# Two layers of a convolution-and-attention trunk: half-row transposes, and low weight parts formed by adding transfers

## The chip, the cores and the metric

The kernel runs on one core of a Trainium2 chip. The metric is the device time of one execution in microseconds (us). The kernel before takes 1127.71 us (median of 3 runs, 1127.39 to 1128.07). A change of less than 0.2%, 2.26 us here, cannot be told from no change by these measurements.

## The reference

The reference is a trunk of two layers over 256 latent tokens and 256 context tokens, 1024 channels wide. One input projection feeds three parts: a gated convolution branch (width 31), neighbourhood attention with 8 heads of 64, and sigmoid gates. A gated sum of the branches goes through an output projection, and a gated feed-forward part with a convolution of width 3 follows. In the second layer the context only gives keys and values. Shortened:

```
p = modulate(rmsnorm(x), sh1, sc1) @ w_in            # GLU | q k v | gates
y_conv = swish(layernorm(dwconv31(a * sigmoid(g)))) @ w_conv_out
s = concat(q k_window + bias, q k_ctx) * scale       # rope on latent q, k
y_attn = (softmax(s) @ concat(v_window, v_ctx)) @ w_na_out
x = x + g1 * ((gate_c * y_conv + gate_a * y_attn) @ w_out)
x = x + g2 * (silu(g) * a) @ w_down                  # a, g = dwconv3(h2 @ w_up)
```

## The kernel before, in words

**Weights and products.** Everything is float32 with almost full accuracy. A weight is split into a rounded high part and a low part, and so is each activation; a product then takes three matmuls for each 128 rows of the contraction (`mm3`, L179 high by high, L180 high by the low activation, L181 low by high). Weights come in units of 128 x 1024 elements (512 KB). `wunit` brings one into a buffer `raw` (four of them, SyncE's queue), ScalarE copies it to `whi` (L160) and VectorE subtracts to make `wlo` (L161); there are four `whi` and four `wlo` buffers. `unit8` cuts the unit into eight weight tiles and `group` runs 24 matmuls over it: 512 columns in layer 0 (latent and context), 256 in most of layer 1.

**Order.** TensorE runs its instructions in the order in which the program writes them. After each group `slot()` gives one step to every generator on the list `side`: one issues convolution taps, one steps the attention, one the layer norm, one the adaptive-norm products; `pace` scales how many steps a slot gives to the last kinds. Between units the attention therefore slips its own matmuls.

**Attention.** For two heads (a pair `j`), `products` forms scores (L440): the two heads lie on partitions 0 to 63 and 64 to 127, so each matmul works on 64 rows, and the two of a pair go to two PSUM banks. The tags are `sc`, `sc`, `pt`, `main`. `scores` takes a maximum on VectorE (L458), an exponential on ScalarE (L461) and a scaling (L464); `ctx_scores` does so for the context's queries (L474, L477, L482). `turn` transposes the normalised scores `pp`, 128 x 128 at a time (L494 latent, L499 context), four of them into each of the four banks, and ScalarE copies each bank into `pT` (L495). `values` multiplies `pT` with V (L512). There are six turns in layer 0 (two of them for the context) and four in layer 1. `step` fixes when a turn, values and products are issued: a turn of one step ago, then the values of the turn before it, then the next products.

**Convolution.** `glu` takes a sigmoid on ScalarE (L606) and a product on VectorE into a padded row `u`; 31 taps for each of four channel groups follow on VectorE (L591, in layer 0 124 taps on 512 columns) into `cb`. Layer 0 has two `u` buffers, so `glu` must finish the taps of group j-2 first. `conv_run` issues two taps a slot in layer 0, three in layer 1. `layer_norm` sums the four groups (L842 and L843 on GpSimd, then one addition on VectorE), multiplies by ones on TensorE (L847), and normalises.

Of the kernel before, what the change touches and what calls it, by code (L numbers as in the profile page):

```python
# [8 lines left out]
F32 = mybir.dt.float32  # L9
# [3 lines left out]
ALU = mybir.AluOpType  # L13
# [32 lines left out]
def trunk(ctx: ExitStack, tc: tile.TileContext, xt, cvec, crow, wall, wada, params, bias_t, rope_t, out):  # L46
# [136 lines left out]
    def group(ps, ws, xh, xl, c):  # L183
# [201 lines left out]
    class Attention:  # L385

        def __init__(self, l, eb, T, V, oh, ol):
            self.l, self.eb, self.T, self.V, self.oh, self.ol = l, eb, T, V, oh, ol  # L390
            self.todo, self.soft, self.pv, self.n, self.at = [], [], [], 0, 0
            self.ctx, self.pairs, self.last = [], 0, None

        def pair(self, j, q, k, bt, last):
            self.pairs, self.last = self.pairs + 1, last
# [9 lines left out]

        def ahead(self, j):

            while any(it[0] <= j for _, _, its in self.todo for it in its):
                self.step(True)

        def run(self):
            while True:
# [3 lines left out]
        def step(self, now=False):  # L416
            self.n += 1
            since = self.n - self.at
            if not now and (since < (4 if self.todo else 3 if self.soft else 2) or not self.todo and self.pairs < 4):
                return  # L420
            if self.todo and not now and self.n - self.todo[0][0] < 2:
                return
            self.at = self.n
# [7 lines left out]
            if self.todo:  # L431
                _, what, its = self.todo.pop(0)
                outs = [self.products(it, [psum(t) for t in tags]) for it, tags in zip(its, (("sc", "sc"), ("pt", "main")))]
                self.soft.append((what, its, [(self.scores if what == LAT else self.ctx_scores)(it, o) for it, o in zip(its, outs)]))

        def product(self, out, q, k, c, d):

# [13 lines left out]
        def scores(self, it, out):  # L451
            qt, bt = it[1], it[-1]
            pps = []
            for i, ps in enumerate(out):

                mx = small([P, 1], "mx")
                p2, b2 = ps.rearrange("p (a k) -> p a k", a=2), bt[:, 2 * qt + i :: 4 - 2 * qt - i, :]
                dve.tensor_tensor_reduce(p2, p2, b2, -1.0, 3.0e38, ALU.add, ALU.min, mx)  # L458
                pp = self.eb.tile([P, 512], F32, tag="pp", bufs=4, name=nm("pp"))
                sm = small([P, 1], "sm")  # L460
                self.exp = act.activation(pp, ps, AF.Exp, bias=mx, scale=-1.0, accum_out=sm)  # L461
                ri = small([P, 1], "ri")
                dve.reciprocal(ri, sm)
                self.done = act.mul(pp, pp, ri)  # L464
                pps.append(pp)
            return pps

        def ctx_scores(self, it, out):
            pps = []
            for ps in out:  # L470
                mx = small([P, 2], "mx2")
                dve.tensor_reduce(mx, ps.rearrange("p (q k) -> p q k", q=2), AX.X, ALU.max, negate=True)
# [12 lines left out]

        def turn(self, what, its, pps):

            pts = [self.eb.tile([P, 4, S], F32, tag="pT", bufs=4, name=nm("pT")) for _ in range(2)]
            for n, tags in enumerate((("sc", "sc"), ("pt", "main"))):
                for i, pp in enumerate(pps[n]):  # L490
                    pt = psum(tags[i])
                    if what == LAT:
                        for kt in range(4):
                            pe.transpose(sl(pt, kt), sl(pp, kt), ident)  # L494
                        act.copy(pts[i][:, :, n * P : (n + 1) * P], pt.rearrange("p (k q) -> p k q", k=4))  # L495
                    else:
                        for t in range(2):
                            for kt in range(2):
                                pe.transpose(pt[:, kt * S + t * P : kt * S + (t + 1) * P], sl(pp, 2 * t + kt), ident)  # L499
                        act.copy(pts[i][:, 2 * n : 2 * n + 2, :], pt.rearrange("p (k q) -> p k q", k=2))  # L500
            js = [its[0][0]] if what == LAT else [it[0] for it in its]
            self.pv.append((what, js, pts))

        def values(self, what, js, pts, bank):
            po = psum(bank)
            kts = range(4) if what == LAT else range(2, 4)
            for n, j in enumerate(js):
                c = slice(n * S, (n + 1) * S)
                for kt in kts:
                    for i in range(2):  # L510
                        h = 2 * j + i
                        pe.matmul(  # L512
                            po[i * HD : (i + 1) * HD, c], self.V[kt][:, h * HD : (h + 1) * HD],
                            pts[i][:, 2 * n + kt - kts[0], :], start=kt == kts[0], stop=kt == kts[-1],
                        )
# [42 lines left out]
    for l in range(DEPTH):  # L558
# [5 lines left out]
        with ExitStack() if last else start as e1a:  # L564
# [5 lines left out]
            NU_ = KC if last else 2  # L570
# [10 lines left out]


            taps = []

            def conv_tap(j, t):
                w = par[:, l * NPAR + DW + j * TAPS + t : l * NPAR + DW + j * TAPS + t + 1]
                src = us[j % NU_][:, :, t : t + S]
                if t == 0:
# [4 lines left out]
            rate = [0]  # L593

            def conv_run():
                while True:
                    for _ in range(rate[0]):
                        if taps:
                            conv_tap(*taps.pop(0))
                    yield  # L600
# [32 lines left out]
            with ExitStack() as e1b:  # L633
                eb = e1b.enter_context(tc.tile_pool(name=f"eb{l}", bufs=1))
                V = [eb.tile([P, CONV], F32, name=f"V{l}_{t}") for t in range(4)]
                att = Attention(l, eb, T, V, oh, ol)

                def v_tile(pv, w, k, toks, parts=range(3)):
                    i = k % 2
# [176 lines left out]
            with ExitStack() as e1c:  # L816
# [15 lines left out]
                def layer_norm():  # L832

                    while taps:
# [17 lines left out]
                    yield  # L852
                    yield
# [10 lines left out]
                    pace[0] = 0.4  # L864

                side.remove(conv)
                ln = layer_norm()
# [357 lines left out]
```

## Time and profile before

| | |
|---|---|
| median of 3 runs | 1127.71 us |
| the profiled execution | 1127.64 us |
| its span in the profile | 1125.9 us (1.74 us lie around it) |
| TensorE busy | 1114.1 us, 99% |
| VectorE, ScalarE, GpSimd busy | 908.3, 563.6, 14.7 us |
| granted TensorE clock | 0.998 |
| layer 0: first groups, attention with taps, gates and branches, feed-forward | 0 to 82, 82 to 198, 198 to 320, 320 to 700 us |
| layer 1: attention with taps, the rest | 745 to 870, 870 to 1116 us |

The profile times every instruction of one execution. PE is TensorE's matmuls, PEld its weight loads, DVE VectorE, ACT ScalarE, POOL GpSimd, SP SyncE. In a timeline the first column is the start, the second the duration, and "x6" joins six like instructions; a matmul's duration contains the way through the array, so what a stream of them costs is read from the distance between starts. A tile's name stands without its number.

### The profile page before, as it was taken

What the parts mean: (1) busy time and instruction counts of PE and PEld (TensorE: products, weight loads), DVE (VectorE), ACT (ScalarE), POOL (GpSimd) and SP (SyncE); (2) the same over time, 40 slices, a digit from 0 to 9 for tenths busy, and PEclk for the clock granted to TensorE, in tenths of its full rate; (3) what the DMA queues carried; (4) which work ended last, traced back from release to release, by engine and by line L of the source; (5) the groups of instructions that cost most, each with busy time, mean ns of one, the idle gap of its engine ahead of it and who ended that gap; (6) DMA issues with size and microseconds to landing.
All of it is one profiled execution on the core that took longest, in us unless ns stands there. A gap on an engine that the chain in (4) does not pass through costs nothing.

```text
span 1125.9 us, 17731 instructions
## 1 busy us (share of the span) xinstructions
PE 1114.1 (99%) x6828; PEld 963.0 (86%) x6828; DVE 908.3 (81%) x1631; ACT 563.6 (50%) x934; POOL 14.7 (1%) x24
## 2 busy tenths in 40 slices
PE   9999999999999999999999999999999999999997
PEld 7778777787789988888888888989888999999997
DVE  5689999685778788888898555789996898988773
ACT  4347657542333543434343222544677667766642
POOL 0000000000000000000000000000000000000000
PEclk9999999999999999999999999999999999999999
DMA  9833231536734354554556665556433575565781
GB/s 364 282 94 103 75 118 38 206 97 214 245 118 138 114 161 150 168 169 149 168 171 215 219 191 186 180 181 187 145 126 121 167 250 163 188 194 181 219 268 58
DMA packets 53941, 190.83 MB, mean 169 GB/s; under 512 B 6240, under 2 KB 6496, under 8 KB 53856
## 3 DMA queue, kind: packets, MB, share of 16 engines
q1 hardware_dynamic: 53568, 189.65, 52.1%
q8 instruction: 54, 0.88, 0.3%
q14 instruction: 31, 0.25, 0.1%
q10 hardware_dynamic: 288, 0.04, 0.0%
HBM read 188.62 MB, written 1.05 MB: 168 GB/s over the span
## 4 chain that ended last, share of the span: by engine, by line
PE 83%; DVE 9%; issue 6%; ACT 2%; DMA 0%; POOL 0%; POOLq 0%; DVEq 0%; SPq 0%; ACTq 0%
PE main L179 24%; PE main L181 24%; PE main L180 24%; DVE cb L591 4%; PE main L644 4%; DVE wlo L161 1%; PE sc L181 1%; PE sc L179 1%; PE sc L180 1%; PE po L202 1%; PE po L512 1%; PE sc L129 1%; PE sc L440 0%; DMA sb<-in_crow 0%; PE sc L494 0%
## 5 line engine op out<-in xcount | busy, mean ns | idle before, releaser
L179 PE MATMUL main<-h,whi 128*128 128x256 f32 (+1 forms) x1328 | 446.7, 337 | 0.0
L181 PE MATMUL main<-h,wlo 128*128 128x256 f32 (+1 forms) x1328 | 442.9, 335 | 1.0 <-DVE wlo L161 1.0
L180 PE MATMUL main<-h,whi 128*128 128x256 f32 (+1 forms) x1328 | 442.2, 334 | 0.1
L160 ACT CAST whi<-raw 128x1024 fp32r<-128x1024 f32 (+1 forms) x244 | 252.3, 1039 | 285.5 <-PE main L180 131.5
L161 DVE TENSOR_TENSOR wlo<-raw,whi 128x1024 fp32r<-128x1024 f32 (+1 forms) x244 | 292.9, 1207 | 112.5 <-ACT whi L160 108.0
L179 PEld LDWEIGHTS main<-h,whi 128*128 128x128 f32 x1328 | 249.4, 188 | 32.1 <-issue 3.6
L181 PEld LDWEIGHTS main<-h,wlo 128*128 128x128 f32 x1328 | 249.3, 188 | 29.6 <-DVE wlo L161 1.5
L180 PEld LDWEIGHTS main<-h,whi 128*128 128x128 f32 x1328 | 249.8, 188 | 28.5 <-DVE h L367 0.5
L591 DVE SCALAR_TENSOR_TENSOR cb<-u,par,cb 128x512 f32<-128x512 f32 (+1 forms) x240 | 140.4, 609 | 1.4
L271 DVE CUSTOM_DVE_ANT_0 t<-raw,sb,par 128x1024 bf16<-128x1024 f32 x100 | 126.7, 1277 | 1.0 <-ACT sb L255 0.7
L179 PE MATMUL main<-fh,whi 128*128 128x256 f32 (+1 forms) x386 | 123.0, 319 | 0.0
L180 PE MATMUL main<-fl,whi 128*128 128x256 f32 (+1 forms) x386 | 122.9, 319 | 0.0
L181 PE MATMUL main<-fh,wlo 128*128 128x256 f32 (+1 forms) x386 | 122.9, 318 | 0.0
L180 PEld LDWEIGHTS main<-fl,whi 128*128 128x128 f32 x386 | 72.7, 188 | 5.6
L179 PEld LDWEIGHTS main<-fh,whi 128*128 128x128 f32 x386 | 72.7, 188 | 5.6
L181 PEld LDWEIGHTS main<-fh,wlo 128*128 128x128 f32 x386 | 72.7, 188 | 5.5
L963 ACT ACTIVATE t<-main,par 128x512 f32<-128x512 f32 (+1 forms) x82 | 50.6, 667 | 39.0 <-PE main L181 39.0
L964 DVE SCALAR_TENSOR_TENSOR t<-main,par,t 128x510 f32<-128x510 f32 (+1 forms) x82 | 47.5, 615 | 10.2 <-ACT t L963 9.8
L967 DVE SCALAR_TENSOR_TENSOR t<-main,par,t 128x510 f32<-128x510 f32 (+1 forms) x82 | 46.6, 609 | 0.0
L366 ACT ACTIVATE h<-t,mod 128x256 fp32r<-128x256 f32 x56 | 25.4, 502 | 36.1 <-DVE t L365 36.1
L898 DVE SCALAR_TENSOR_TENSOR x<-main,mod,x 128x256 f32<-128x256 f32 x48 | 22.1, 479 | 23.5 <-PE main L181 23.3
L644 PE MATMUL main<-whi,h 128*128 128x512 f32 x128 | 40.6, 402 | 0.1
(221 smaller groups left out, 1188.2 us busy)
## 6 DMA issues: line engine op xcount, KB each, us to landing
raw<-in_wall SPq DMA_DIRECT2D x239, 512.0 KB, 4.2
raw<-in_wada SPq DMA_DIRECT2D x88, 512.0 KB, 4.3
bias<-in_bias_t SPq DMA_DIRECT2D x8, 640.0 KB, 4.8
row<-in_wada SPq DMA_DIRECT2D x8, 512.0 KB, 4.7
sb<-in_crow SPq DMA_DIRECT2D x5, 512.0 KB, 6.0
x<-in_xt SPq DMA_DIRECT2D x8, 256.0 KB, 4.4
raw<-in_wall SPq DMA_DIRECT2D x8, 256.0 KB, 7.1
out<-t SPq DMA_DIRECT2D x3, 256.0 KB, 2.1
```

Of the source, the lines that this page charges most:

```text
L160: act.copy(hi[:, c], r[:, c])
L161: dve.tensor_tensor(lo[:, c], r[:, c], hi[:, c].bitcast(F32), ALU.subtract)
L179: pe.matmul(ps, w[0], xh, start=start, stop=False)
L180: pe.matmul(ps, w[0], xl, start=False, stop=False)
L181: pe.matmul(ps, w[1], xh, start=False, stop=stop)
L271: dve.tensor_tensor_reduce(tmp().bitcast(BF16), r, v, 1.0, pr(l, BADA + n, 1), ALU.mult, ALU.add, mods[l][:, n, s : s + 1])
L366: high = act.activation(hi[:, c], y[:, c], AF.Identity, bias=b)
L591: dve.scalar_tensor_tensor(cb[j], src, w, cb[j], ALU.mult, ALU.add)
L644: mm = pe.matmul(pv[t], h1[n == 1][k][:, c], w[n == 2][:, b], start=k + n == 0, stop=k == KD - 1 and n == 2)
L963: act.activation(c, pv_, AF.Identity, bias=pr(l, FDB + t, 1), scale=w[1])
L964: dve.scalar_tensor_tensor(c[:, :, 1:], pv_[:, :, : S - 1], w[0], c[:, :, 1:], ALU.mult, ALU.add)
L967: dve.scalar_tensor_tensor(c[:, :, : S - 1], pv_[:, :, 1:], w[2], c[:, :, : S - 1], ALU.mult, ALU.add)
```

## The change

1. *Low parts.* A new `wadded` serves 19 units of layer 0 (the first 19 input-projection units after the first group's) and 7 of layer 1. ScalarE copies the high part as before (L199 in the new file) and writes its negative into `wlo` (L200); GpSimd's queue then issues a DMA that adds `raw` onto `wlo` (L201). VectorE's subtraction falls away for these units.
2. *Turning on row halves.* `turn` issues each transpose as two, one on rows 0 to 63 and one on rows 64 to 127, with 64 columns each, into two PSUM banks (L520 latent and context). A bank now holds one half of both heads, and ScalarE copies two banks (L523) into one `pT` tile.
3. *Order of the attention.* In layer 0 a turn with no values ahead of it stands alone: its products are issued at a later slot (`alone`, `late`).
4. *Tied taps.* Each tap is placed behind the latest maximum (`after`). Layer 0 has four `u` buffers, and three taps a slot.
5. *Sigmoid behind copies.* In layer 0 `glu_groups` first has the attention issue what is ripe, and puts its sigmoid behind the last copy of a turn.
6. *Row sums.* In layer 0 the two additions of L842 and L843 move to VectorE, the pace of the layer norm is 0.6 instead of 1.0 and 0.4, and it yields four times instead of twice behind the squares.
7. The kernel sets a scratch size for descriptors of 1024.

```diff
+ADDED = {*((0, U_IN + i) for i in range(19)), *((1, U_IN + i) for i in (7, 8, 9, 14, 15, 16, 17))}
...
+    def wadded(l, u):
+
+        r = raw_unit(wall[l, u])
+        hi = wp.tile([P, UW], F32R, tag="whi", bufs=4, name=nm("whi"))
+        lo = wp.tile([P, UW], F32R, tag="wlo", bufs=4, name=nm("wlo"))
+        act.copy(hi, r)
+        act.mul(lo, hi.bitcast(F32), -1.0)
+        pool.dma_start(lo, r, accum_op=ALU.add)
+        return hi, lo
...
-        w = wunit(l, u, at)
+        w = wadded(l, u) if (l, u) in ADDED else wunit(l, u, at)
...
+            alone = not self.l and self.soft and not self.pv and not self.late
...
+            if self.late:
+                self.late, self.at = False, self.n
+                return self.issue()
+            if alone and not now:
+                self.late = True
...
-            pts = [self.eb.tile([P, 4, S], F32, tag="pT", bufs=4, name=nm("pT")) for _ in range(2)]
+            pT = self.eb.tile([P, 2, 4, S], F32, tag="pT", bufs=2, name=nm("pT"))
             for n, tags in enumerate((("sc", "sc"), ("pt", "main"))):
+                outs = [psum(t).rearrange("p (i s q) -> p i s q", i=2, s=4) for t in tags]
                 for i, pp in enumerate(pps[n]):
-                    pt = psum(tags[i])
+                    for s in range(4):
+                        src = s if what == LAT else s % 2 * 2 + s // 2
+                        for pt, r in zip(outs, HALF):
+                            pe.transpose(pt[:, i, s], sl(pp, src)[r], ident[r, r])
+                for pt, r in zip(outs, HALF):
                     if what == LAT:
-                        for kt in range(4):
-                            pe.transpose(sl(pt, kt), sl(pp, kt), ident)
-                        act.copy(pts[i][:, :, n * P : (n + 1) * P], pt.rearrange("p (k q) -> p k q", k=4))
+                        self.copied = act.copy(pT[:, :, :, n * P + r.start : n * P + r.stop], pt)
...
             def conv_tap(j, t):
+                if after[0] is not None:
+                    with tc.issue_after(after[0].ins):
+                        tap(j, t)
+                else:
+                    tap(j, t)
...
-                glu(j, pa, pg)
+                copied = None if last else att.ahead(j - 2)
+                with tc.issue_after(copied.ins) if copied else ExitStack():
+                    glu(j, pa, pg)
...
-                rate[0] = 3 if last else 2
+                rate[0] = 3 if last else 3.0
...
-                    pace[0] = 1.0
+                    pace[0] = 1.0 if last else 0.6
...
-                    pool.tensor_tensor(sm[:, :T], flat[0], flat[1], ALU.add)
-                    pool.tensor_tensor(sm[:, :T], sm[:, :T], flat[2], ALU.add)
+                    eng = pool if last else dve
+                    eng.tensor_tensor(sm[:, :T], flat[0], flat[1], ALU.add)
+                    eng.tensor_tensor(sm[:, :T], sm[:, :T], flat[2], ALU.add)
```

**Where instructions move, first place.** TensorE's order at the first turn of layer 0, before: the second unit's last matmuls, the turn, and directly behind it the second pair of products.

```order
L181 MATMUL main_972<-h_189,wlo_975 128x512
L494 MATMUL sc_1009<-ident,pp_845 128x128 x4
L494 MATMUL sc_1015<-ident,pp_853 128x128 x4
L494 MATMUL pt_1021<-ident,pp_861 128x128 x4
L494 MATMUL main_1027<-ident,pp_869 128x128 x4
L440 MATMUL sc_1033<-qk_967,qk_921 128x512
L440 MATMUL sc_1034<-qk_967,qk_921 128x512
```

The same turn after (its first six and last two rows of 32), then a whole unit of 24 matmuls, and only then the products.

```order
L182 MATMUL main_945<-h_189,wlo_949 128x512
L520 MATMUL sc_984<-ident,pp_861 128x64
L520 MATMUL sc_985<-ident,pp_861 128x64
L520 MATMUL sc_984<-ident,pp_861 128x64
L520 MATMUL sc_985<-ident,pp_861 128x64
...
L520 MATMUL pt_1004<-ident,pp_885 128x64
L520 MATMUL main_1005<-ident,pp_885 128x64
L180 MATMUL main_1035<-h_182,whi_1038 128x512
...
L182 MATMUL main_1035<-h_189,wlo_1039 128x512
L465 MATMUL sc_1073<-qk_1030,qk_940 128x512
```

Sixteen transposes have become sixteen pairs with half the columns, whose partners go to different banks, and the turn stands one unit earlier, between two units.

**Second place.** ScalarE's order at the first turn of layer 1, before: three casts of later units and a rotary copy, then the four copies of the turn.

```order
L160 CAST whi_7497<-raw_7496 128x1024
L160 CAST whi_7541<-raw_7540 128x1024
L768 ACTIVATE qk_7333<-t_7327 128x256
L160 CAST whi_7674<-raw_7673 128x1024
L495 COPY pT_7373<-sc_7375 128x4x128
L495 COPY pT_7374<-sc_7381 128x4x128
L495 COPY pT_7373<-pt_7387 128x4x128
L495 COPY pT_7374<-main_7393 128x4x128
```

The same place after: two of the three units are made by adding, so that a negative (L200) follows each of their casts, one of them directly ahead of the copies.

```order
L199 CAST whi_7631<-raw_7629 128x1024
L161 CAST whi_7675<-raw_7674 128x1024
L200 ACTIVATE wlo_7632<-whi_7631 128x1024
L807 ACTIVATE qk_7450<-t_7444 128x256
L199 CAST whi_7824<-raw_7822 128x1024
L200 ACTIVATE wlo_7825<-whi_7824 128x1024
L523 COPY pT_7490<-sc_7491 128x8x64
L523 COPY pT_7490<-sc_7492 128x8x64
L523 COPY pT_7490<-pt_7511 128x8x64
```

One more instruction stands between the cast and the copies, and each copy of an `sc` bank now needs both heads' transposes.

**Third place.** GpSimd's queue in layer 1 after; before, it held only the two additions (L842, L843) here.

```order
L201 DMA wlo_7195<-raw_7192 128x1024
L201 DMA wlo_7233<-raw_7230 128x1024
L201 DMA wlo_7374<-raw_7371 128x1024
L201 DMA wlo_7412<-raw_7409 128x1024
L201 DMA wlo_7594<-raw_7591 128x1024
L882 TENSOR_TENSOR ss_8479<-cb_0_6603,cb_1_6604 128x256
L201 DMA wlo_7632<-raw_7629 128x1024
L201 DMA wlo_7825<-raw_7822 128x1024
L883 TENSOR_TENSOR ss_8479<-ss_8479,cb_2_6605 128x256
```

The seven transfers are interleaved with the two additions of the row sums, in the order in which the queue issues them.

More of the change, by code (lines that the diff above doesn't have):

```diff
@@ L385, in trunk, with __init__ @@
     class Attention:
-        def __init__(self, l, eb, T, V, oh, ol):
+        def __init__(self, l, eb, T, V, oh, ol, after):
+            self.after = after
             self.l, self.eb, self.T, self.V, self.oh, self.ol = l, eb, T, V, oh, ol
             self.todo, self.soft, self.pv, self.n, self.at = [], [], [], 0, 0
-            self.ctx, self.pairs, self.last = [], 0, None
+            self.ctx, self.pairs, self.last, self.late = [], 0, None, False
         def pair(self, j, q, k, bt, last):
@@ L406, in ahead @@
         def ahead(self, j):
+            self.copied = None
             while any(it[0] <= j for _, _, its in self.todo for it in its):
                 self.step(True)
+            return self.copied
         def run(self):
@@ L418, in step @@
             since = self.n - self.at
-            if not now and (since < (4 if self.todo else 3 if self.soft else 2) or not self.todo and self.pairs < 4):
+            alone = not self.l and self.soft and not self.pv and not self.late
+            if not now and since < (4 if self.todo or alone else 3 if self.soft else 2) and not self.late:
                 return
-            if self.todo and not now and self.n - self.todo[0][0] < 2:
+            if not now and not alone and not self.todo and self.pairs < 4:
                 return
+            if not now and not alone and self.todo and self.n - self.todo[0][0] < 2:
+                return
+            if self.late:
[3 more added lines that the diff above has]
+                self.late = True
             self.at = self.n
@@ L430, in step, with issue @@
                 self.values(*work, "sc" if work[0] == CTX and not (soft or self.todo) else "po")
[L431 to L434, printed above, removed]
+            if self.todo and not self.late:
+                self.issue()
+        def issue(self):
+            _, what, its = self.todo.pop(0)
+            outs = [self.products(it, [psum(t) for t in tags]) for it, tags in zip(its, (("sc", "sc"), ("pt", "main")))]
+            self.soft.append((what, its, [(self.scores if what == LAT else self.ctx_scores)(it, o) for it, o in zip(its, outs)]))
         def product(self, out, q, k, c, d):
@@ L486, in turn, with values @@
         def turn(self, what, its, pps):
-            pts = [self.eb.tile([P, 4, S], F32, tag="pT", bufs=4, name=nm("pT")) for _ in range(2)]
+            pT = self.eb.tile([P, 2, 4, S], F32, tag="pT", bufs=2, name=nm("pT"))
             for n, tags in enumerate((("sc", "sc"), ("pt", "main"))):
+                outs = [psum(t).rearrange("p (i s q) -> p i s q", i=2, s=4) for t in tags]
                 for i, pp in enumerate(pps[n]):
-                    pt = psum(tags[i])
+                    for s in range(4):
[3 more added lines that the diff above has]
+                for pt, r in zip(outs, HALF):
                     if what == LAT:
-                        for kt in range(4):
-                            pe.transpose(sl(pt, kt), sl(pp, kt), ident)
-                        act.copy(pts[i][:, :, n * P : (n + 1) * P], pt.rearrange("p (k q) -> p k q", k=4))
-                    else:
[L497 to L500, printed above, removed]
+                        self.copied = act.copy(pT[:, :, :, n * P + r.start : n * P + r.stop], pt)
+                    else:
+                        to = pT[:, :, 2 * n : 2 * n + 2].rearrange("p i k (t q) -> p i (k t) q", t=2)
+                        self.copied = act.copy(to[:, :, :, r], pt)
             js = [its[0][0]] if what == LAT else [it[0] for it in its]
-            self.pv.append((what, js, pts))
-        def values(self, what, js, pts, bank):
+            self.pv.append((what, js, [pT[:, i] for i in range(2)]))
+        def values(self, what, js, pT, bank):
             po = psum(bank)
@@ L513, in values @@
                             po[i * HD : (i + 1) * HD, c], self.V[kt][:, h * HD : (h + 1) * HD],
-                            pts[i][:, 2 * n + kt - kts[0], :], start=kt == kts[0], stop=kt == kts[-1],
+                            pT[i][:, 2 * n + kt - kts[0]], start=kt == kts[0], stop=kt == kts[-1],
                         )
@@ L569, in trunk @@
             rope = ea.tile([P, 2, S], F32, name=f"rope{l}")
-            NU_ = KC if last else 2
+            NU_ = KC
             us = [ea.tile([P, NS, S + 2 * PAD], F32, name=f"u{l}_{i}") for i in range(NU_)]
@@ L583, in trunk, with tap @@
             taps = []
+            after = [None]
             def conv_tap(j, t):
+                if after[0] is not None:
[3 more added lines that the diff above has]
+                    tap(j, t)
+            def tap(j, t):
                 w = par[:, l * NPAR + DW + j * TAPS + t : l * NPAR + DW + j * TAPS + t + 1]
@@ L591, in conv_tap @@
                     dve.scalar_tensor_tensor(cb[j], src, w, cb[j], ALU.mult, ALU.add)
-            rate = [0]
+            rate = [0.0]
             def conv_run():
+                due = 0.0
                 while True:
-                    for _ in range(rate[0]):
+                    due += rate[0]
+                    while due >= 1:
+                        due -= 1
                         if taps:
@@ L635, in trunk @@
                 V = [eb.tile([P, CONV], F32, name=f"V{l}_{t}") for t in range(4)]
-                att = Attention(l, eb, T, V, oh, ol)
+                att = Attention(l, eb, T, V, oh, ol, after)
                 def v_tile(pv, w, k, toks, parts=range(3)):
@@ L851, in layer_norm @@
                         s2.add(flat[j], j == KC - 1)
-                    yield
-                    yield
+                    for _ in range(2 if last else 4):
+                        yield
                     pb = yield from rstd(s2, CONV, "po")
@@ L863, in layer_norm @@
                         yield
-                    pace[0] = 0.4
+                    pace[0] = 0.4 if last else 0.6
                 side.remove(conv)
```

6 lines of the change are left out of this document (3 added, 3 removed).

## The prediction

> **What bounds the kernel now.** I read the busy shares first, then what TensorE waits for, then the busy time by stage, and last the distances between matmul starts. The page's busy line:
>
> ```profile
> span 1125.9 us, 17731 instructions
> PE 1114.1 (99%) x6828; PEld 963.0 (86%) x6828; DVE 908.3 (81%) x1631; ACT 563.6 (50%) x934; POOL 14.7 (1%) x24
> ```
>
> The reader should see that TensorE (PE) is busy for all but 11.8 us. The view of waits, for TensorE's queue, complete:
>
> ```profile
> PE sc L129 <- POOL ident masks.py:199: 1.8, 1, 1.8
> PE main L181 <- DVE wlo L161: 1.0, 2, 0.6
> PE pt L1094 <- DVE t L314: 0.7, 1, 0.7
> PE po L1102 <- DVE rs L1099: 0.6, 1, 0.6
> PE pt L228 <- ACT t L221: 0.6, 1, 0.6
> PE po L351 <- POOL rs L346: 0.4, 1, 0.4
> ```
>
> These are 5.1 us in seven waits, and the only one on a low part made by VectorE is 1.0 us. Two stretches of attention, of layer 0 and layer 1, the columns being PE, PEld, DVE, ACT, POOL, clock, DMA share, GB/s:
>
> ```profile
> 82.00:100.00 18.00, 18.00 (x84) 14.13 (x83) 17.62 (x43) 11.77 (x21) 0.00 (x0) 1.00 0.22 78
> 810.00:830.00 20.00, 20.00 (x144) 16.85 (x142) 20.00 (x53) 15.20 (x31) 0.00 (x0) 1.00 0.52 161
> ```
>
> VectorE is full there, but so is TensorE, and TensorE hardly waits: VectorE's filling is convolution taps, which nothing needs soon. So taking work off VectorE is worth little, at most the 1.0 us of the second row above. What moves the time is **how long TensorE's own list takes**, and that list changes only in the turns.
>
> **The turn, before.** TensorE in layer 1's first turn:
>
> ```profile
> 809.56 0.39 PE L181 MATMUL main<-h,wlo 128*128 128x512 f32 x1
> 809.79 1.04 PE L494 MATMUL sc<-ident,pp 128*128 128x128 f32 x8
> 810.66 0.60 PE L494 MATMUL pt<-ident,pp 128*128 128x128 f32 x4
> 811.10 0.60 PE L494 MATMUL main<-ident,pp 128*128 128x128 f32 x4
> 811.63 1.16 PE L440 MATMUL sc<-qk,qk 64*128 64x512 f32 x6
> ```
>
> Eight transposes take 810.66 - 809.79 = 0.87 us, 0.109 us each; sixteen take 1.74 us, and ten turns 17.4 us. That is all that halving can act on.
>
> **What a half pair costs.** The weight loads by form (busy us, then mean ns):
>
> ```profile
> L494 PEld LDWEIGHTS sc<-ident,pp 128*128 128x128 f32 x64 | 7.4, 141 | 0.8
> L440 PEld LDWEIGHTS main<-qk,qk 64*128 64x128 f32 x36 | 6.0, 185 | 0.2
> L512 PEld LDWEIGHTS po<-pT,V 128*64 128x64 f32 x144 | 9.5, 136 | 5.4 <-issue 1.3
> L179 PEld LDWEIGHTS main<-h,whi 128*128 128x128 f32 x1328 | 249.4, 188 | 32.1 <-issue 3.6
> ```
>
> Loads of 128 and 64 columns take 188 and 136 ns, so 52 ns for 64 columns and some 84 ns fixed. 64 rows with 128 columns take 185: half the rows do not shorten a load. A transpose's load, 141 ns, is 57 ns above the fixed part. A half transpose keeps its 128 weight columns (some 57 ns) and has 64 moving columns instead of 128 (half of 109, 55 ns). So a pair costs about 0.059 us if its two halves run beside each other, twice that if not. Whether they do, the context products show, which are pairs of 64 rows with loads of 64 x 128:
>
> ```profile
> 114.75 0.28 PE L440 MATMUL main<-qk,qk 64*128 64x256 f32 x1
> 114.75 0.28 PE L440 MATMUL pt<-qk,qk 64*128 64x256 f32 x1
> 114.87 0.28 PE L440 MATMUL main<-qk,qk 64*128 64x256 f32 x1
> 114.87 0.28 PE L440 MATMUL pt<-qk,qk 64*128 64x256 f32 x1
> ...
> 115.35 0.28 PE L440 MATMUL main<-qk,qk 64*128 64x256 f32 x1
> ```
>
> Both start together, a pair each 0.12 us. The two loads (185 - 84 = 101 ns each) fit into 0.12 us only side by side. No row shows transposes so, nor a pair closer than 0.12 us; the ends are 0.055 (half of 0.109) and 0.12 us. I take **0.059**, since both resources that I could read give it. Saved: 16 x (0.109 - 0.059) = 0.80 a turn, **8.0 us in ten**. The ends give +8.6 and -1.8.
>
> By the Trainium skill, TensorE: Matmul & The Clock Gate, section "Wait — 56ns, not 53.3ns?", starts are never closer than about 25 ns, and with a sequencer that decodes in software about 62 ns a matmul bind instead. By the first a pair could be 0.05 and the sum stands; by the second it would be 0.124, the case of the first rival below. The rows above, two matmuls in 0.12 us, exclude neither.
>
> **Changing between whole array and halves.** Layer 0's first products, between two units:
>
> ```profile
> 81.67 0.39 PE L180 MATMUL main<-h,whi 128*128 128x512 f32 x1
> 81.90 0.40 PE L181 MATMUL main<-h,wlo 128*128 128x512 f32 x1
> 82.23 0.97 PE L440 MATMUL sc<-qk,qk 64*128 64x512 f32 x6
> 83.04 0.39 PE L440 MATMUL main<-qk,qk 64*128 64x512 f32 x1
> ...
> 83.83 0.50 PE L179 MATMUL main<-h,whi 128*128 128x512 f32 x1
> 84.16 0.40 PE L180 MATMUL main<-h,whi 128*128 128x512 f32 x1
> ```
>
> From 81.90 to 84.16 are eight steps (a whole one, six pairs, a whole one), at the undisturbed 0.23 us (81.67 to 81.90) 1.84 us; 2.26 are spent, so some 0.2 us to enter and 0.2 to leave. Before, a turn was whole and its products had to enter; now the turn enters. Where values (whole rows) stand between turn and products, both now enter. I count 0.25 us for nine turns and 0.2 for layer 0's first, which now stands alone: **-2.4 us** (ends: 0, if the short matmuls hide it, and 10 x 0.4 = 4).
>
> **Copies behind a negative.** ScalarE at layer 1's first turn:
>
> ```profile
> 809.76 1.05 ACT L160 CAST whi<-raw 128x1024 fp32r<-128x1024 f32 x1 [1.35 <-PE main L180]
> 810.71 1.06 ACT L495 COPY pT<-sc 128x512 f32<-128x512 f32 x2
> 811.66 0.60 ACT L495 COPY pT<-pt 128x512 f32<-128x512 f32 x1
> ```
>
> The cast waits for a weight buffer that the last L180 before the turn frees. After, the negative follows it. I price it as a second cast, 1.05 us (no row shows it; at 0.6, a copy's, the wait is half a us shorter). The `sc` copies then run 811.85 to 812.90 instead of to 811.77. The products, which write the `sc` banks, are ready at 809.79 + 0.2 + 16 x 0.059 = 810.9 and wait some 2.0 us: **-1.9 us**, once. Layer 0's turns have the same order, but there either a unit of 24 matmuls (5.5 us) or the values cover the copies; -0.2 together. If all four turns of layer 1 stalled so, it would be -6.
>
> **Adding transfers.** The tightest unit is the second of layer 1's seven in TensorE's order, number 7 of the list. Its cast before, and the first row of its successor, 24 matmuls later:
>
> ```profile
> 779.85 1.05 ACT L160 CAST whi<-raw 128x1024 fp32r<-128x1024 f32 x1 [0.37 <-PE main L180]
> 788.35 0.28 PE L179 MATMUL main<-h,whi 128*128 128x256 f32 x1
> 788.59 0.28 PE L181 MATMUL main<-h,wlo 128*128 128x256 f32 x1
> 791.19 0.39 PE L179 MATMUL main<-h,whi 128*128 128x512 f32 x1
> ```
>
> 788.35 to 788.59 are two steps of 0.12 us, and 24 of them before 791.19 the unit begins, at 788.35, so its first L181 is that at 788.59; the cast ended at 780.90. After the negative (781.95), 6.6 us remain for the transfer. No row shows an adding one, or any issued by GpSimd. The page's nearest, with KB and us to landing:
>
> ```profile
> raw<-in_wall SPq DMA_DIRECT2D x239, 512.0 KB, 4.2
> ```
>
> Plain 512 KB take 4.2 us; two reads for one write make 8.4 the upper end. I take 6 (between them, nearer to the plain row): nothing waits. At 8.4 this unit is 1.8 us late. Layer 0's units have over 12 us each. By the Trainium skill, DMA: Bandwidth & Descriptors, section "Anatomy of one DMA — SWDGE (gpsimd) path", a transfer of GpSimd takes about 2.0 us plus its bytes at 436 GB/s, an estimate of 3.2 us here; by that nothing waits either, and no run here shows it.
>
> **The rest.** VectorE loses 26 subtractions of 1.2 us and gains two additions of about 0.65 us; ScalarE gains 26 x 1.05 us where it is a third idle. Tied taps, three taps a slot, the sigmoid and the row sums reorder work that TensorE does not wait for; I cost them at nothing, hidden by TensorE's units. Of the 1.0 us on `wlo` and the 0.6 us behind `t L221`, in the table of waits, I count a third as gone with the freer VectorE: **+0.5**.
>
> **Sum.** +8.0 - 2.4 - 1.9 - 0.2 + 0.5 = +4.0 us saved. Against the profiled execution, 1127.64 us (span 1125.9 and 1.74 around it), that is **1123.6 us**; the median, 1127.71, stands 0.07 higher.
>
> **Rivals.**
>
> 1. *Half transposes are no cheaper in pairs* (slower side). Each matmul costs a fixed 0.055 to 0.06 us of issue, as the closest rows (ten in 0.60 us) allow. A pair then takes 0.109 to 0.12: the 8.0 becomes 0 to -1.8, and the entering and the copies remain: 1131.6 to 1133.4, say **1132**. It decides from a pair of 0.084 us on, where 160 x 0.025 = 4.0 is used up. Against it: both loads and streams, read by themselves, need under 0.06. If partners even ran one after another at 0.109, it would be 17 us more, 1149.
> 2. *Late adds.* At 8.4 us or more that unit waits 1.8 us, and with VectorE full and transfers queued it could be 10 us, so 3.4 for it and 1 to 2 for the units next to it: 1125.5 to 1129, **about 1127.5**: no change.
> 3. *More gain.* If entering costs nothing where the matmuls are short, and the copies wait less (a negative of 0.6 us), 2.4 + 0.5 more: **about 1120.5**.
> 4. *The change does not do what it says*: adds or halves run as before. The halves are in TensorE's list, so this is only the case of rival 1.
>
> **Chances and range.** Forecast (1121.5 to 1125.4) 0.50; rival 3, below it, 0.13; rival 2, 0.15, spread over no change; rival 1, 0.19; others, 0.03. Faster by over 0.2% (under 1125.4; 2.26 us is about what the measurement can tell) 0.64, within 0.2% 0.16, slower 0.20. The range leaves out the farthest of rivals 1 and 3: 1119.5 to 1132.
>
> **What would show it.** In the changed profile: starts of half transposes of one bank 0.059 us apart (0.11 refutes the largest term); a gap of 0.1 us in front of each turn; in layer 1's first turn a gap of some 2 us on TensorE behind the transposes, ended by the copy L523; TensorE's waits on `wlo` without a row for L201's transfers; transfers of 512 KB from GpSimd's queue in about 6 us. The forecast is wrong if partners do not overlap, or if these transfers take over 8 us.

## The result, and the profile after

The changed kernel takes 1125.12 us (median of 9 runs, 1124.23 to 1126.18) against 1127.71 us before (9 runs, 1127.2 to 1128.42). The ratio is 0.9977, with a 95% interval of 0.9967 to 0.9987: faster by 0.23%, on the edge of what can be told. The profiled execution takes 1124.46 us, with a span of 1122.7 us and a clock of 0.998. The busy line and the waits of TensorE, after:

```profile
span 1122.7 us, 18139 instructions
PE 1110.2 (99%) x6988; PEld 955.8 (85%) x6988; DVE 887.7 (79%) x1607; ACT 588.9 (52%) x960; POOL 36.5 (3%) x50
```

```profile
PE sc L130 <- POOL ident masks.py:199: 1.8, 1, 1.8
PE main L182 <- DVE wlo L162: 1.8, 3, 0.8
PE sc L465 <- ACT pT L523: 1.0, 2, 0.8
PE pt L1134 <- DVE t L325: 0.7, 1, 0.7
PE po L1142 <- DVE rs L1139: 0.6, 1, 0.6
```

VectorE is busy for 20.6 us less, ScalarE for 25.3 us more. TensorE has a new wait, 1.0 us on the copies of two turns (L523), and waits longer on low parts that VectorE makes. Nothing waits on an adding transfer; the page's row for them, KB and us to landing:

```profile
wlo<-raw POOLq DMA_DIRECT2D x26, 512.0 KB, 5.6
```

Layer 1's first turn, TensorE's timeline:

```profile
807.97 0.40 PE L182 MATMUL main<-h,wlo 128*128 128x512 f32 x1
808.29 0.71 PE L520 MATMUL sc<-ident,pp 64*128 64x64 f32 x16
808.84 0.22 PE L520 MATMUL main<-ident,pp 64*128 64x64 f32 x1
808.84 0.22 PE L520 MATMUL pt<-ident,pp 64*128 64x64 f32 x1
808.90 0.22 PE L520 MATMUL main<-ident,pp 64*128 64x64 f32 x1
808.91 0.23 PE L520 MATMUL pt<-ident,pp 64*128 64x64 f32 x1
...
809.31 0.71 PE L465 MATMUL main<-qk,qk 64*128 64x512 f32 x2
810.83 1.22 PE L465 MATMUL sc<-qk,qk 64*128 64x512 f32 x5 [0.81 <-ACT pT L523]
```

Partners start together, and a pair follows each 0.06 to 0.07 us (eight pairs from 808.29 to 808.84). The turn is entered 0.32 us behind the last full matmul instead of 0.23. Over the ten turns, from the matmul ahead to the one behind, a turn took 2.07 us before (0.23 + 1.64 + 0.20, first to last start in the middle) and takes 1.47 us where values follow (0.33 + 0.99 + 0.15). **That is 0.60 us a turn.** The second turn of layer 0 is the exception: it takes 1.33 us in the middle, because it waits inside for a scaled score. ScalarE beside layer 1's first turn:

```profile
808.16 1.05 ACT L199 CAST whi<-raw 128x1024 fp32r<-128x1024 f32 x1 [0.30 <-PE main L181]
809.24 1.06 ACT L200 ACTIVATE wlo<-whi 128x1024 fp32r<-128x1024 f32 x1
810.21 1.06 ACT L523 COPY pT<-sc 128x512 f32<-128x512 f32 x2
```

Cast, negative and copies follow one another, and the products of the `sc` banks start behind the first copy, at 810.83, with the turn over since 809.3. Two products ran ahead, since `main` has four banks.

Where the time came from: the same weight load of the three-matmul products (there are 5796 in both traces) was looked up in both, and its start after is set against its start before.

```
stretch (times of before)                     us after less us before
six turns of layer 0, to 196                  -2.2
a wait of TensorE at 209, gone                -0.8
210 to 351: gates, branches, low parts late   +1.3
layer 1's first turn                          +0.9
layer 1's other three turns                   -1.8
a wait at 937, gone                           -0.3
the end, behind the last weight load          -0.3
sum                                           -3.2
```

Ten turns would be -6.0. Layer 0's six gave -2.2 instead of -3.6, since the second and the third gave nothing, and layer 1's first cost 0.9 instead of giving 0.6.

### The profile page after: what moved, and what is told of

Same layout as the page of the kernel before. It is cut to its first block, busy times and chain, and to the rows that moved or that the text cites. A ratio compares the mean times of both kernels' runs of the same rounds, so it can differ in the third digit from the quotient of the medians.

```text
span 1122.7 us, 18139 instructions
## 1 busy us (share of the span) xinstructions
PE 1110.2 (99%) x6988; PEld 955.8 (85%) x6988; DVE 887.7 (79%) x1607; ACT 588.9 (52%) x960; POOL 36.5 (3%) x50
## 4 chain that ended last, share of the span: by engine, by line
PE 88%; issue 5%; DVE 4%; ACT 2%; POOL 0%; POOLq 0%; DVEq 0%; ACTq 0%
PE main L180 25%; PE main L182 25%; PE main L181 25%; PE main L683 4%; DVE cb L625 2%; PE po L538 1%; PE sc L182 1%; PE sc L180 1%; PE sc L181 1%; PE po L213 1%; PE sc L465 1%; PE sc L130 1%; PE sc L213 0%; PE pt L465 0%; PE sc L520 0%
## 5 line engine op out<-in xcount | busy, mean ns | idle before, releaser
L161 ACT CAST whi<-raw 128x1024 fp32r<-128x1024 f32 (+1 forms) x218 | 225.3, 1037 | 256.6 <-DMA raw<-in_wall 137.4
L162 DVE TENSOR_TENSOR wlo<-raw,whi 128x1024 fp32r<-128x1024 f32 (+1 forms) x218 | 262.2, 1208 | 98.9 <-ACT whi L161 96.9
L625 DVE SCALAR_TENSOR_TENSOR cb<-u,par,cb 128x512 f32<-128x512 f32 (+1 forms) x240 | 144.2, 614 | 3.2
L1029 ACT CAST fh<-t 128x256 fp32r<-128x256 f32 (+1 forms) x43 | 21.9, 510 | 34.9 <-DVE t L1019 34.5
```

Of the source, the lines that this page charges most:

```text
L161: act.copy(hi[:, c], r[:, c])
L162: dve.tensor_tensor(lo[:, c], r[:, c], hi[:, c].bitcast(F32), ALU.subtract)
```

## Experiments

The theory after the result: TensorE's list is the time, each turn is worth 0.60 us, and what is missing went into new waits for copies. The rival: the adds, by relieving VectorE, carry the gain, and the halves are used up by entering. All times are medians; the kernel before took 1127.99 to 1128.05 us beside them, 0.3 us more than beside the changed kernel's 1125.12, so differences from the changed kernel are good to some tenths.

**1. Halves alone.** The kernel before with the new `turn`.

```diff
-            pts = [self.eb.tile([P, 4, S], F32, tag="pT", bufs=4, name=nm("pT")) for _ in range(2)]
+            pT = self.eb.tile([P, 2, 4, S], F32, tag="pT", bufs=2, name=nm("pT"))
...
+                            pe.transpose(pt[:, i, s], sl(pp, src)[r], ident[r, r])
```

> The kernel before with only the half-row turning. Theory (TensorE's own list is the time): each of ten turns with its entry takes 0.60 us less, as in the changed kernel's profile (2.07 to 1.47 us), so 1127.7 - 6.0 = 1121.7 us, plus up to 1.5 us where products now wait for copies that need both heads: 1121.7 to 1123.2. Rival (the gain is VectorE's relief by the adds, and entering uses the halves up): 1127.7 us, no change.

Measured: 1129.09 us, ratio 1.0014 (1.0005 to 1.0023). The theory fails, since nothing is gained. The loss of 0.14% lies below the 0.2% that can be told, so the rival's number, no change, may stand, but not its reason: the transposes and the entering take as long as in the changed kernel. Its waits of TensorE, the new ones, and the stretch at layer 0's last turn by 2 us (PE, PEld, DVE, ACT, POOL, clock, DMA share, GB/s):

```profile
PE sc L440 <- ACT pT L498: 1.3, 3, 0.8
PE pt L495 <- ACT pp L482: 1.1, 1, 1.1
...
PE po L513 <- DVE ol L520: 0.7, 1, 0.7
```

```profile
187.00:189.00 2.00, 2.00 (x11) 1.53 (x9) 1.88 (x5) 2.00 (x7) 0.00 (x0) 1.00 0.12 49
189.00:191.00 2.00, 0.97 (x18) 0.58 (x16) 1.96 (x5) 2.00 (x10) 0.00 (x0) 1.00 0.00 0
191.00:193.00 2.00, 1.66 (x18) 1.14 (x20) 1.93 (x5) 1.98 (x6) 0.00 (x0) 0.85 0.00 0
193.00:195.00 2.00, 2.00 (x12) 1.05 (x12) 1.93 (x3) 1.99 (x3) 0.00 (x0) 0.50 0.00 0
195.00:197.00 2.00, 2.00 (x12) 1.18 (x9) 1.90 (x3) 2.00 (x6) 0.00 (x0) 0.80 0.00 0
```

The second half of this turn waits 1.1 us for a scaled score, and then the granted clock falls to 0.50 for 3.4 us. By the weight loads this one stretch costs 3.2 us, and the rest of the kernel gains 2.3. The softmax is late because of VectorE: the turn's first exponential here waits 5.52 us for a maximum, where the same row of the kernel before waits 3.21 (shown in experiment 5).

```profile
185.30 0.48 ACT L477 ACTIVATE pp<-sc,mx 128x256 f32<-128x256 f32 x1 [5.52 <-DVE mx L472]
```

That maximum starts 4.1 us behind the last of its turn's products, with taps and a subtraction ahead of it in VectorE's queue; before, it started 1.6 us behind them (table in experiment 6). With 1.6 us here too it would come 2.5 us earlier, more than the whole wait. So this wait is not what the old turn's length had covered, but the order of VectorE's queue. The smaller waits for copies (L498) fit what the length had covered; that was not tried by itself.

**2. Whole transposes in the changed kernel** (the old `turn`, the rest as changed).

```diff
-                            pe.transpose(pt[:, i, s], sl(pp, src)[r], ident[r, r])
+                            pe.transpose(sl(pt, kt), sl(pp, kt), ident)
```

> The changed kernel with whole transposes as before. Theory: the 6.0 us of the turns come back, less up to 1.5 us of waits for copies: 1129.6 to 1131.1 us, slower than before. Rival (VectorE's relief is the gain): 1125.1 us, as the changed kernel.

Measured: 1128.38 us, ratio 1.0005 (0.9996 to 1.0014): no change against before, and neither expectation. The halves are worth some 3.3 us in the changed kernel, where the theory said 4.5 to 6.0. Its wait on copies (L523's counterpart) is gone from the table of waits.

**3. No adds in the changed kernel.**

```diff
+ADDED = set()
```

> The changed kernel with no unit made by adding (all low parts by VectorE's subtraction). Theory: the negatives ahead of the turns' copies are gone, so layer 1's first turn waits 1.1 us less and layer 0's copies some tenths less: 1123.2 to 1124.2 us. Rival (the adds carry the gain): 1127 us or more, as VectorE, full in the attention, gets 31 us back.

Measured: 1128.33 us, ratio 1.0001 (0.9992 to 1.001). The rival's number. The theory's own step came true all the same: at layer 1's first turn TensorE's wait for the copies is 0.2 us instead of 0.8, and the stretch gives 0.8 us back.

```profile
PE sc L465 <- ACT pT L523: 0.2, 1, 0.2
```

More is lost elsewhere. Against the changed kernel's trace 2.7 us are lost up to the unit behind layer 0's second products, which start at 104.21 instead of 102.20. Part of this is another order: ten of the first turn's sixteen values now stand ahead of these products. (So TensorE's list is not always in the order in which the program writes; the scheduler that lays out the queues had moved them.) Then TensorE waits 0.5 us for the rotary copy L807, which had waited 3.30 us for VectorE (L802). The ten values are missing later, but behind the second turn 2.3 us are still lost; that turn waits 0.6 us for a scaled score. So the relief of VectorE matters, though TensorE hardly waited for it in the kernel before.

```profile
102.22 1.51 PE L538 MATMUL po<-pT,V 128*64 128x256 f32 x10
104.21 0.50 PE L465 MATMUL sc<-qk,qk 64*128 64x512 f32 x2 [0.48 <-ACT qk L807]
```

```profile
101.78 0.39 ACT L807 ACTIVATE qk<-main 128x256 fp32r<-128x256 f32 x1 [3.30 <-DVE t L802]
```

**4. One unit less by adding** (number 17 of layer 1).

```diff
+ADDED = {*((0, U_IN + i) for i in range(19)), *((1, U_IN + i) for i in (7, 8, 9, 14, 15, 16))}
```

> The changed kernel with one unit less made by adding: number 17 of layer 1, whose negative stands directly ahead of the copies of layer 1's first turn. Theory: that negative's 1.06 us leaves the chain cast, negative, copies, products, so the wait of 1.1 us on TensorE there goes to about 0: 1124.1 us, 1.0 below the changed kernel. Rival (the wait comes from the bank that now needs both heads, not from the negative): 1125.1 us.

Measured: 1125.78 us, ratio 0.9978 (0.997 to 0.9987), as the changed kernel. The negative is gone, but a rotary copy, which itself waited 0.70 us for VectorE, took its place ahead of the copies, and TensorE's wait there grew from 0.8 to 1.3 us:

```profile
810.65 1.92 PE L465 MATMUL sc<-qk,qk 64*128 64x512 f32 x6 [1.33 <-ACT pT L523]
```

By itself this settles nothing between bank and negative: taking one instruction from a queue lets another in. Experiments 1 and 3 say more. In both the bank needs both heads and no negative exists, and TensorE waits 0.24 us for these copies, against 0.81 in the changed kernel. Most of the wait comes from what stands ahead of the copies on ScalarE.

**5. Adds alone.** The kernel before with `wadded` and its 26 units.

```diff
+        w = wadded(l, u) if (l, u) in ADDED else wunit(l, u, at)
```

> The kernel before with only the 26 low parts made by adding (and the scratch size). Theory now (halves and adds gain only together, because VectorE's relief shortens the chains that the shorter turns uncover): TensorE's list is as long as before and nothing waited for VectorE, so 1127.2 to 1128.5 us, no change. Rival (the adds gain by themselves): the 3.2 us by which the kernel without adds lay above the changed one, so 1124.5 us.

Measured: 1133.34 us (6 runs, 1130.2 to 1136.91), ratio 1.0047 (1.003 to 1.0063). Slower by 5 us: both expectations fail. ScalarE's first exponential at layer 0's last turn, here and then in the kernel before, with what it waited for:

```profile
188.16 0.47 ACT L488 ACTIVATE pp<-sc,mx 128x256 f32<-128x256 f32 x1 [5.29 <-DVE mx L483]
```

```profile
184.09 0.47 ACT L477 ACTIVATE pp<-sc,mx 128x256 f32<-128x256 f32 x1 [3.21 <-DVE mx L472]
```

VectorE's queue, with the kernel with adds first:

```profile
184.21 2.32 DVE L602 SCALAR_TENSOR_TENSOR cb<-u,par,cb 128x512 f32<-128x512 f32 x3
186.44 0.42 DVE L530 TENSOR_TENSOR ol<-po,oh 128x256 fp32r<-128x256 f32 x1
186.78 0.75 DVE L602 SCALAR_TENSOR_TENSOR cb<-u,par,cb 128x512 f32<-128x512 f32 x1
187.44 1.29 DVE L483 TENSOR_REDUCE mx<-sc 128x2 f32<-128x512 f32 x2
```

```profile
181.73 0.73 DVE L591 SCALAR_TENSOR_TENSOR cb<-u,par,cb 128x512 f32<-128x512 f32 x1
182.39 0.41 DVE L519 TENSOR_TENSOR ol<-po,oh 128x256 fp32r<-128x256 f32 x1
182.72 0.73 DVE L591 SCALAR_TENSOR_TENSOR cb<-u,par,cb 128x512 f32<-128x512 f32 x1
183.39 1.27 DVE L472 TENSOR_REDUCE mx<-sc 128x2 f32<-128x512 f32 x2
```

The freed time was filled with taps, three instead of one here, ahead of the work on which the softmax hangs, and VectorE works through them in that order. TensorE waits 1.9 us at layer 1's first turn, 1.6 us at this one, and 1.0 us on adding transfers:

```profile
PE sc L451 <- ACT pT L506: 1.9, 1, 1.9
...
PE pt L510 <- ACT pp L493: 1.6, 1, 1.6
...
PE main L182 <- DMA wlo<-raw: 1.0, 2, 0.9
```

**6. Taps not tied** in the changed kernel.

```diff
-                if after[0] is not None:
+                if False:
```

> The changed kernel with taps not tied to the maxima. Theory: tied taps keep VectorE's maxima and rotary operations ahead of the taps; without the tie the exponentials come later in layer 0, the turns wait by some tenths each: 1125.5 to 1127 us. Rival (the tie does nothing, VectorE has room): 1125.1 us.

Measured: 1130.74 us, ratio 1.0027 (1.0018 to 1.0036), worse than expected. The same thing as in 5, TensorE's largest waits:

```profile
PE sc L465 <- ACT pT L523: 3.4, 2, 3.3
...
PE pt L520 <- ACT pp L507: 1.8, 1, 1.8
```

The clock falls to 0.50 at both: behind the wait of 1.8 us, and 2 us into the one of 3.3 us. The profiled execution is the slowest of the eleven, 1135.52 us, so these waits are larger than what the median lost. The delay of the maxima at layer 0's last turn, from the timelines of TensorE and VectorE:

| kernel | last of its products starts | first maximum starts | us between |
|---|---|---|---|
| before | 181.81 | 183.39 | 1.6 |
| halves alone (1) | 180.49 | 184.60 | 4.1 |
| adds alone (5) | 182.59 | 187.44 | 4.8 |
| changed, taps not tied (6) | 180.85 | 185.84 | 5.0 |
| changed | 180.25 | 180.77 | 0.5 |

So **the ties keep the maxima ahead of the taps**; where they are missing, neither the halves nor the adds gain.

**7. Row sums and pace as before** in the changed kernel.

```diff
-                    pace[0] = 1.0 if last else 0.6
+                    pace[0] = 1.0
...
-                    eng = pool if last else dve
+                    eng = pool
```

> The changed kernel with the row sums of layer 0 on GpSimd and the layer norm's pace as before. Theory (the pace's change is what delays a subtraction at 277 us, by 0.9 us, and takes away the 0.7 us wait at 209): the 0.3 us that the changed kernel lost between 199 and 284 us come back: 1124.8 us, not to be told from the changed kernel. Rival (row sums and pace carry part of the gain): 1126.5 us or more.

Measured: 1129.76 us, ratio 1.0011 (1.0003 to 1.002): the rival, and by more than it said. The largest single wait, 1.7 us, is on a layer norm's sum. With a pace of 1.0 the sums come into TensorE's list some 2.4 us sooner behind the products of the row sums, and VectorE makes them 3.5 us later, behind a subtraction that waits 2.23 us for its cast. GpSimd had finished its row sums by 174 us, so it is not what held them; the pace and the yields were not parted.

```profile
PE main L182 <- DVE wlo L162: 2.1, 3, 1.1
...
PE pt L347 <- DVE ss L333: 1.7, 1, 1.7
PE pt L239 <- ACT t L232: 1.1, 1, 1.1
```

**8 and 9. The lone first turn, and the sigmoid.** Each is undone in the changed kernel.

```diff
-            alone = not self.l and self.soft and not self.pv and not self.late
+            alone = False
```

> The changed kernel with layer 0's first turn directly ahead of the second products, as before, instead of alone. Theory (a short turn no longer covers the cast, the negative and the copies): the copies end 1.9 us behind the turn in the changed kernel's profile, so the products would wait that long, less 0.4 us for one change of mode saved, and 1.7 us more where the clock drops behind it: 1126.6 to 1128.5 us. Rival (the lone turn costs a change of mode and brings nothing): 1124.7 us.

```diff
-                with tc.issue_after(copied.ins) if copied else ExitStack():
-                    glu(j, pa, pg)
+                glu(j, pa, pg)
```

> The changed kernel with the sigmoid of layer 0's gated groups where the scheduler puts it, not behind the copies. Theory: where its table load and itself (1.28 and 0.5 us) come ahead of a turn's copies, the context products of the second turn, which wait 0.8 us for them now, wait up to 2.6 us: 1126 to 1129 us with the clock's drop. Rival (the sigmoid never stood ahead of copies that anyone waits for): 1125.1 us.

Measured: 1125.5 us (0.998, 0.9971 to 0.9989) and 1125.45 us (0.9975, 0.9966 to 0.9984); the changed kernel beside them took 1125.02. Neither can be told from the changed kernel; the times of the theory failed in both. Its waits are there, but small: without the lone turn the products wait 0.8 us for its copies, and the net by the weight loads is 0.4 us; with the sigmoid free, the second turn's products wait 0.98 us for the copies instead of 0.15.

**10 to 12. Copies first.** A unit whose buffer is freed just ahead of a turn (four units on) is cast behind that turn's last copy, and so are the rotary copies of a group that ran beside it. It was run twice, the second time with the changed kernel beside it.

```diff
+            turned[units[0] + 4] = self.copied
...
+        with tc.issue_after(turned[units[0]].ins) if units[0] in turned else ExitStack():
+            act.copy(hi, r)
+            act.mul(lo, hi.bitcast(F32), -1.0)
```

> The changed kernel with ScalarE's order changed: the unit whose buffer is freed just ahead of a turn is cast behind that turn's copies, and so are the rotary copies of a group that ran beside the turn. Theory: TensorE's waits for the copies (1.1 us at layer 1's first turn, 0.8 us at layer 0's second, 0.4 us at its third) shrink to 0.5 us in all, and the clock's drop behind a wait of over 1 us, 1.7 us where it comes, goes too: 1122.5 to 1123.5 us. Rival (the waits only move to the casts or to the exponentials): 1125 us or more.

> The changed kernel unchanged, to be set beside the next on one chip: 1125.1 us, with runs between 1124.2 and 1126.2.

> The changed kernel with the unit of the freed buffer and the rotary copies cast behind the turns' copies, a second time, beside the changed kernel itself: 1.1 us below it, as in the two profiles (1123.3 against 1124.5), so 1124.0 us; the rival is that the two are the same, 1125.1.

Measured: 1124.30 us, ratio 0.9965 (0.9953 to 0.9977), and 1124.26 us, 0.9968 (0.9955 to 0.998); the changed kernel beside the second 1125.02 us, 0.9976 (0.9966 to 0.9985). The medians are 0.8 us apart both times, which is below the 0.2% that can be told, and the intervals overlap; so it is likely, not certain, that this version beats the changed kernel; it beats the one before. The part of the theory on the wait is shown, TensorE's wait on the copies having gone from 1.0 to 0.2 us:

```profile
PE sc L472 <- ACT pT L530: 0.2, 1, 0.2
```

The time expected, 1122.5 to 1123.5, was too low: the gates' stretch waits as before, and the 1.7 us of a clock drop were not there to be won: the changed kernel's two profiles have no drop at a turn, and its mean clock was 0.997 or 0.998 in every run.

Not taken out one by one were the four `u` buffers and the three taps a slot of change 4, and the yields of change 6; what they carry stays open.

## Why the prediction was right

The time lies in the range, 1.5 us above the forecast of 1123.6: 2.6 us were saved where 4.0 were forecast. The two largest terms held, one was mis-sized, and the price of nothing for the rest came out by luck.

1. *The halves* (8.0 less 2.4 for entering, so 5.6 us). Right: 6.0 us. A pair takes 0.066 us (0.99 us over 15 steps) instead of 0.059 (the two readings behind that had given 0.057 and 0.055), and entering and leaving cost less than the 0.25 us a turn that I had charged: 0.33 instead of 0.23 us ahead, 0.15 instead of 0.20 behind. The first rival, a fixed cost of each matmul, is refuted: 32 matmuls start in 1.0 us. By the Trainium skill, TensorE: Matmul & The Clock Gate, section "Wait — 56ns, not 53.3ns?", a sequencer that decodes in software takes some 62 ns a matmul, and starts are never closer than about 25 ns. The first does not bind here, at 33 ns a matmul on average; the second does not hold for partners, which start within 0.01 us of each other.
2. *Copies behind a negative* (-1.9 us in layer 1, -0.2 in layer 0). The mechanism was right. Layer 1's first turn lost 1.5 us (from the 0.6 saved to 0.9 lost). Layer 0's term was **mis-sized**: its second and third turn lost 0.5 to 0.8 us each, 1.4 us with the others, because cast and negative stand ahead of those copies too and the values do not cover them (in the second, 0.35 us of it is the wait inside the turn). Experiment 10, with the copies first, gives 0.65 and 0.50 us of this back by the weight loads, and 0.8 us at layer 1's first turn.
3. *Adding transfers* in 6 us, nothing waits. Right: 5.6 us, and no wait on them in the changed kernel; the estimate of 3.2 us that stands beside it in the prediction was too short.
4. *The rest at nothing, since TensorE does not wait for VectorE.* **This step failed as an argument, and that the sum did not feel it was luck.** Taken out of the changed kernel, the adds, the ties and the row sums with their pace cost 3.2, 5.6 and 4.6 us (3, 6, 7), and the adds alone cost 5 us (5). That hardly anything waits for a full engine was true of one order of its queue, and the change alters that order; the parts repair one another's damage, which the prediction did not foresee.
5. *Small waits, +0.5 us.* The waits at 209 and 937 went (1.1 us), but subtractions came late at 277 and the stretch from 210 to 351 lost 1.3: about -0.2.

Together 6.0 - 1.5 - 1.4 - 0.2 + 0.3 (the end) = 3.2 us between the profiles, 2.6 between the medians, where 4.0 was forecast.

## What to carry to other kernels

When the bound engine's own work is shortened, look at what its old length covered: the copies beside it did not get shorter, and half the gain became waits. An engine that is full of filler but waited for by nobody is not free: here VectorE's queue put taps ahead of the maxima in every version without ties, whether the change had shortened TensorE's work or VectorE's. Test a bundle by taking each part out and by putting each in alone; here the halves alone gained nothing, the adds alone cost 5 us, and both together without the ties cost 2.7 us.

## What the runs showed of the hardware

- **TensorE's clock falls to one half behind a wait, though not behind every one.** In experiment 1 a wait of 1.1 us was followed by 3.4 us at 0.50; so were 1.3 us in experiment 4, 1.6 us in 5, 1.8 us in 6 and 1.7 us in 7. In experiment 6 a wait of 3.3 us had 6.8 us at 0.50, which began 2.1 us into it. Two waits of 1.1 us in experiment 7 (at 208 and 241 us) had none behind them, nor had 1.9 us at layer 1's first turn in experiment 5:

```profile
816.00:818.00 2.00, 0.20 (x2) 0.00 (x0) 2.00 (x4) 2.00 (x4) 0.86 (x1) 1.00 0.00 0
818.00:820.00 2.00, 1.93 (x12) 1.32 (x12) 2.00 (x8) 1.48 (x4) 0.00 (x0) 1.00 0.68 125
```

  A drop costs about 1.7 us (3.4 at half speed), as much as the wait ahead of it or more. The Trainium skill, TensorE: Matmul & The Clock Gate, section "HAM oscillation — how this bites in real kernels", warns of idle gaps of over about 3.4 us; here gaps of a third to a half of that came ahead of drops. One program can have drops in one execution and not in the next: of the six of adds alone, the three with a mean clock of 0.998 took 1130.2 to 1132.2 us, the three with 0.993 to 0.996 took 1134.5 to 1136.9. What decides between the cases was not tried.
- Two half transposes, of 64 rows each on the two row halves, run beside each other, a pair in 0.066 us where a 128 x 128 one takes 0.109, and a load for a transpose of 64 rows takes 139 ns against 141 for 128.
- A 512 KB adding transfer from one buffer on the core to another takes 5.6 us to land, against 4.2 us for a plain load.
